# Two-layer decoder trunk on one core: the low halves of the query weights and of two up-weight chunks move from VectorE to GpSimd

## Chip, cores and metric

One core of one Trainium2 chip runs the whole kernel. The metric is device time in microseconds for one launch. The unchanged kernel was measured three times: median 3047.41 us (3045.8 to 3048.99).

## The reference, cut to what matters

512 tokens of width 1024 go through two layers. Each layer is a mixer (three parallel head groups, then an output projection added to x) and then a PEER block: 16384 one-neuron experts, of which each token uses 128, chosen by eight product-key heads.

```
x = x + mixed @ w_out[i]
xn = rmsnorm(x, norm_ffn[i])
q = (xn @ w_q)                      # 1024 x 2048: 16 blocks of 128 columns
s1, s2 = q halves against keys1, keys2      # 128 keys each
v1, i1 = top_k(s1, 16); v2, i2 = top_k(s2, 16)
... 16 best sums per head -> experts, gates = softmax
h = gelu(u[experts] . xn)           # u: 128 chunks of 128 experts
x = x + sum(gates * h * v[experts])
```

## The kernel before, in words

Products that must be exact to float32 are made of three passes on TensorE (`mm3`, L75 to L77): high times high (L75), high times low (L76), low times high (L77). So each weight block of 128x1024 is split in two: ScalarE rounds it to the high half (`uh`, L650), VectorE subtracts that from the block for the low half (`ul`, L651). Only L77 reads `ul`.

At the end of a layer's mixer, TensorE makes the output projection (`pso`) block of 128 tokens by block. For each block VectorE adds the result to x (L369), ScalarE takes the sum of squares (`sq`, L173), VectorE works out the reciprocal root in a chain of twelve 128x1 instructions (L161 to L168) and scales the block (`xn`, L185), TensorE transposes it (`psn`, L189), and ScalarE and VectorE split it again (`ahi`, L191; `alo`, L192). The last add and norm, those of tokens 384 to 511, are the generator `rest`, which the PEER part starts.

The PEER part loads three of the sixteen query blocks (numbered c = -16 to -14), splits them, and runs them at once against the first 256 tokens (`qmm`, `psq` of 128x256), while the norm of the last tokens is still under way. Then it goes through the sixteen query blocks: half or all of the product, scores against the keys (`pss`, L677), and on VectorE `best` (L892 to L896: the 16 best of 128 for each token, four blocks of tokens, some 80 instructions for each query block). The same stream of blocks then goes on with c = 0, 1, ... 127, the chunks of u (`hidden`, `psh` of 128x384); `uraw`, `uh` and `ul` have three buffers each. From there VectorE also does the routing (`route`), the gate matrices, and the rows of the last token block, which GpSimd gathers (L735).

The order on each engine is set by a scheduler, which orders by readiness and priority. What is wrapped in `pin` (`keep_in_program_order`) keeps the order of the program among the pinned instructions of its own engine. The `uh` and `ul` of the first three query blocks are pinned, and so is the last add of x:

```python
            split_u(-NQ)
            split_u(1 - NQ)
            split_u(2 - NQ)
            next(rest)          # tc.keep_in_program_order(add(*late))
            first = [self.psA.tile([P, T], F32, tag="a", name="psq") for _ in range(3)]
            for j in range(3):
                qmm(j, first[j], slice(0, T // 2))
            next(rest, None)    # norm of the last 128 tokens
```

So on VectorE that add (L369) stands behind three `ul`. An engine takes its instructions strictly in its own order.

Of the kernel before, what the change touches and what calls it, by code (L numbers as in the profile page):

```python
# [7 lines left out]
F32 = mybir.dt.float32  # L8
F32R = mybir.dt.float32r
# [5 lines left out]
OP = mybir.AluOpType  # L15
# [4 lines left out]
P = 128  # L20
# [3 lines left out]
KD = D // P  # L24
# [14 lines left out]
NUW = 3  # L39
# [24 lines left out]
class K:  # L64
# [562 lines left out]
    def peer(self, L, xh, xl, rest):  # L627
        nc, tc, ins = self.nc, self.tc, self.ins
        G = self.dr.tile([NCH // GE, P, TD // TBAT, GE * TBAT], F32, tag="G", name="G")
        H = self.dr.tile([NPRE, P, TD], F32, tag="H", name="H")  # L630
        with ExitStack() as pc:
# [6 lines left out]
            pin = tc.keep_in_program_order  # L638
            gt, us, uw, vs, hs = {}, {}, {}, {}, {}
# [6 lines left out]
                    us[c] = self.up.tile([P, KD, P], F32, tag="uraw", name="uraw", bufs=NUR)  # L646
                    pin(nc.sync.dma_start(us[c], ins["peer_u"][L, c] if c >= 0 else ins["peer_w_q"][L, c + NQ]))

            def split(hi, lo, src, pin=pin):
                pin(nc.scalar.copy(hi, src))  # L650
                self.last = pin(nc.vector.tensor_tensor(lo, src, hi.bitcast(F32), op=OP.subtract))  # L651
                return hi, lo

            def split_u(c, pin=pin):
                if c < NCH:
                    uw[c] = split(self.up.tile([P, KD, P], F32R, tag="uh", name="uh", bufs=NUW),
                                  self.up.tile([P, KD, P], F32R, tag="ul", name="ul", bufs=NUW), us.pop(c), pin)

            def hidden(c, pin=pin):
                uh, ul = uw.pop(c)  # L660
# [30 lines left out]
            for j in range(3):  # L691
                load_u(j - NQ)
# [3 lines that stand above are left out]
            next(rest)  # L696
            first = [self.psA.tile([P, T], F32, tag="a", name="psq") for _ in range(3)]
# [371 lines left out]
```

## Time and profile before

| what | value |
|---|---|
| median of 3 runs | 3047.41 us |
| profiled execution, its own time | 3044.03 us |
| its span | 3042.3 us |
| TensorE busy | 2971.3 us, 98% |
| VectorE busy | 2443.7 us, 80% |
| ScalarE busy | 1268.9 us, 42% |
| GpSimd busy | 736.2 us, 24% |
| mean granted TensorE clock | 0.993 |

All times within the program are microseconds from the start of the span. The PEER part of layer 0 begins at about 286, that of layer 1 at about 1796. A granted clock of 1.00 stands for 2.4 GHz and 0.50 for 1.2 GHz; a value between them is a window that holds some of both.

### The profile page before, as it was taken

Reading aid. Unit: us, or ns where it says so; the run is one execution under the profiler, and the core shown is the slowest. Engines: PE = TensorE matmul, PEld = TensorE weight load, DVE = VectorE, ACT = ScalarE, POOL = GpSimd, SP = SyncE. Lnnn points to the kernel's source line nnn. Section 1 sums busy time; section 2 is a strip of 40 time slices with the busy share of each in tenths; the row PEclk is TensorE's granted clock in tenths of the full one; section 3 lists DMA queues with packets and bytes.
Section 4 is the critical chain, followed back from the end, with each engine's and each line's share of the span. In section 5 each row is a group of like instructions: output and inputs, shape, how many; then the busy total and the mean of one; then the engine's idle time right before and its main releaser. Section 6 shows DMA issues by size and latency. Waiting matters only on the chain.

```text
span 3042.3 us, 45583 instructions
## 1 busy us (share of the span) xinstructions
PE 2971.3 (98%) x16742; PEld 2659.7 (87%) x16742; DVE 2443.7 (80%) x5057; ACT 1268.9 (42%) x1874; POOL 736.2 (24%) x553
## 2 busy tenths in 40 slices
PE   7999999999999999999999999999999999999998
PEld 7977889999999998788889788999999999988886
DVE  5766999987788787877766769999868788878777
ACT  5343346556333333333353533555553333323333
POOL 0000000222455544322100000002225555542221
PEclk9999999999999999999999999999999999999999
DMA  4212247799989888999722212578999899889996
GB/s 122 67 58 70 98 143 255 271 307 335 348 321 333 322 324 309 362 335 330 282 78 67 73 65 96 169 242 295 314 351 335 323 321 338 330 295 353 333 348 232
DMA packets 335696, 756.64 MB, mean 249 GB/s; under 512 B 31568, under 2 KB 192240, under 8 KB 331376
## 3 DMA queue, kind: packets, MB, share of 16 engines
q1 hardware_dynamic: 141936, 406.60, 37.2%
q0 software_dynamic: 73728, 268.47, 24.7%
q10 hardware_dynamic: 119808, 78.66, 8.2%
q8 instruction: 131, 2.15, 0.3%
q14 instruction: 93, 0.76, 0.1%
HBM read 672.89 MB, written 80.74 MB: 248 GB/s over the span
## 4 chain that ended last, share of the span: by engine, by line
PE 79%; DVE 6%; issue 4%; ACT 4%; DMA 3%; POOL 2%; ACTq 1%; SPq 0%; POOLq 0%; DVEq 0%
PE pv L77 10%; PE pv L76 10%; PE pv L75 10%; PE psh L75 9%; PE psh L77 9%; PE psh L76 9%; PE psp L77 2%; PE psp L76 2%; PE psp L75 2%; PE psq L76 2%; PE psq L77 2%; PE psq L75 2%; POOL row L735 2%; DMA row<-in_v_rows,idx 1%; ACTq L789 1%
## 5 line engine op out<-in xcount | busy, mean ns | idle before, releaser
L735 POOL DMA_INDIRECT row<-in_u_rows,idx x256 | 389.1, 1520 | 1326.3 <-DVE si L893 679.3
L75 PE MATMUL psh<-ahi,uh 128*128 128x384 f32 x2048 | 694.5, 339 | 10.1 <-ACT ht L665 10.1
L77 PE MATMUL psh<-ahi,ul 128*128 128x384 f32 x2048 | 689.2, 337 | 6.6 <-DVE ul L651 6.6
L76 PE MATMUL psh<-alo,uh 128*128 128x384 f32 x2048 | 688.4, 336 | 0.0
L75 PE MATMUL pv<-vh,wh 128*128 128x512 f32 x1536 | 597.7, 390 | 10.4 <-ACT wh L835 10.4
L77 PE MATMUL pv<-vh,wl 128*128 128x512 f32 x1536 | 600.4, 391 | 0.0
L76 PE MATMUL pv<-vl,wh 128*128 128x512 f32 x1536 | 599.9, 391 | 0.0
L735 POOL DMA_INDIRECT row<-in_v_rows,idx x256 | 329.1, 1286 | 604.1 <-DVE yacc L752 568.3
L650 ACT CAST uh<-uraw 128x1024 fp32r<-128x1024 f32 x288 | 302.7, 1053 | 319.8 <-PE psh L76 154.4
L651 DVE TENSOR_TENSOR ul<-uraw,uh 128x1024 fp32r<-128x1024 f32 x288 | 350.4, 1220 | 98.9 <-ACT uh L650 85.5
L75 PEld LDWEIGHTS psh<-ahi,uh 128*128 128x128 f32 x2048 | 387.1, 189 | 16.2 <-ACT ht L665 11.9
L77 PEld LDWEIGHTS psh<-ahi,ul 128*128 128x128 f32 x2048 | 386.6, 189 | 7.2 <-DVE ul L651 7.2
L76 PEld LDWEIGHTS psh<-alo,uh 128*128 128x128 f32 x2048 | 387.0, 189 | 4.1
L821 DVE TENSOR_TENSOR vl<-vraw,vh 128x1024 fp32r<-128x1024 f32 x256 | 312.5, 1221 | 86.5 <-issue 66.5
L665 ACT ACTIVATE ht<-psh 128x384 f32<-128x384 f32 x256 | 125.3, 489 | 613.6 <-PE psh L77 601.1
L75 PEld LDWEIGHTS pv<-vh,wh 128*128 128x128 f32 x1536 | 288.9, 188 | 69.3 <-ACT wh L835 12.0
L77 PEld LDWEIGHTS pv<-vh,wl 128*128 128x128 f32 x1536 | 288.9, 188 | 61.6 <-DVE wl L821 1.1
L76 PEld LDWEIGHTS pv<-vl,wh 128*128 128x128 f32 x1536 | 289.0, 188 | 58.6 <-DVE vl L821 0.5
L752 DVE SCALAR_TENSOR_TENSOR yacc<-row,wk,yacc 128x1024 f32<-128x1024 f32 x254 | 325.7, 1282 | 11.0 <-DMA row<-in_v_rows,idx 9.5
L743 DVE SCALAR_TENSOR_TENSOR gscr<-row,xg 128x1024 f32<-128x1024 f32 x256 | 312.5, 1221 | 13.0 <-DMA row<-in_u_rows,idx 11.3
L835 ACT CAST wh<-ht 128x384 fp32r<-128x384 f32 x256 | 130.7, 510 | 383.2 <-PE pv L76 236.3
L826 ACT CAST vh<-vraw 128x1024 fp32r<-128x1024 f32 x256 | 268.7, 1050 | 26.6 <-DMA vraw<-in_v_rows 24.5
(289 smaller groups left out, 4406.8 us busy)
## 6 DMA issues: line engine op xcount, KB each, us to landing
uraw<-in_peer_u SPq DMA_DIRECT2D x256, 512.0 KB
vraw<-in_v_rows SPq DMA_DIRECT2D x256, 512.0 KB
G<-stg ACTq DMA_DIRECT2D x48, 1024.0 KB
g<-G SPq DMA_DIRECT2D x32, 1536.0 KB
H<-ht ACTq DMA_DIRECT2D x144, 192.0 KB
ht<-H SPq DMA_DIRECT2D x144, 192.0 KB
wraw<-in_w_in SPq DMA_DIRECT2D x96, 256.0 KB
uraw<-in_peer_w_q SPq DMA_DIRECT2D x32, 512.0 KB
```

Of the source, the lines that this page charges most:

```text
L75: mm(ps, ah, bh, start=first, stop=False)
L76: mm(ps, ah, bl, start=False, stop=False)
L77: mm(ps, al, bh, start=False, stop=last)
L650: pin(nc.scalar.copy(hi, src))
L651: self.last = pin(nc.vector.tensor_tensor(lo, src, hi.bitcast(F32), op=OP.subtract))
L665: pin(nc.scalar.activation(hs[c], ps, AF.Gelu))
L735: nc.gpsimd.indirect_dma_start(out=r, out_offset=None, in_=ins[name], in_offset=bass.IndirectOffsetOnAxis(ap=idx[:, k:k + 1], axis=0))
L743: nc.vector.scalar_tensor_tensor(sc, r, 1.0, xg, op0=OP.mult, op1=OP.mult, accum_out=hd[:, k:k + 1])
L752: nc.vector.scalar_tensor_tensor(yacc, r, wk[:, k:k + 1], yacc, op0=OP.mult, op1=OP.add)
L821: self.last = pin(nc.vector.tensor_tensor(lo, src, hi.bitcast(F32), op=OP.subtract))
L826: pin(nc.scalar.copy(vh[c], vs[c]))
L835: pin(nc.scalar.copy(wh[c], hs[c]))
```

## The change

`split` takes the engine of the subtraction as an argument, and `split_u` gives GpSimd for c below 2: the sixteen query blocks and the u chunks 0 and 1. That is 18 subtractions in each layer, 36 in all. ScalarE still makes the high halves.

```diff
-            def split(hi, lo, src, pin=pin):
+            def split(hi, lo, src, pin=pin, eng=nc.vector):
                 pin(nc.scalar.copy(hi, src))
-                self.last = pin(nc.vector.tensor_tensor(lo, src, hi.bitcast(F32), op=OP.subtract))
+                self.last = pin(eng.tensor_tensor(lo, src, hi.bitcast(F32), op=OP.subtract))
                 return hi, lo
...
-                                  self.up.tile([P, KD, P], F32R, tag="ul", name="ul", bufs=NUW), us.pop(c), pin)
+                                  self.up.tile([P, KD, P], F32R, tag="ul", name="ul", bufs=NUW), us.pop(c), pin,
+                                  nc.gpsimd if c < 2 else nc.vector)
```

On GpSimd the 18 instructions of a layer stand in one row between the last memset of the mixer and the first gather. SyncE's order doesn't change. On VectorE the 18 are gone, and all others stand in the order they had. On VectorE at the start of the PEER part (layer 0; layer 1 alike), where `x<-x,pso` is the add of the last 512 columns of the last tokens:

```order
 L369 TENSOR_TENSOR x<-x,pso 128x512
 L192 TENSOR_TENSOR alo<-psn,ahi 128x4x128 x2
-L651 TENSOR_TENSOR ul<-uraw,uh 128x1024 x3
 L369 TENSOR_TENSOR x<-x,pso 128x512
 L161 TENSOR_SCALAR rv<-ss 128x1
```

The last add no longer stands behind three subtractions. On ScalarE at the same place, where `sq` is the sum of squares of the last tokens and the three `uh` are the first query blocks:

```order
 L173 ACTIVATE sq,ss<-x 128x1024
 L191 CAST ahi<-psn 128x4x128 x2
+L173 ACTIVATE sq,ss<-x 128x1024
 L650 CAST uh<-uraw 128x1024 x3
-L173 ACTIVATE sq,ss<-x 128x1024
 L191 CAST ahi<-psn 128x4x128 x2
 L650 CAST uh<-uraw 128x1024
```

The scheduler now puts the sum of squares ahead of the three high halves instead of behind them. On TensorE, at the first query block, where `psn` is a transpose of the last tokens' `xn`:

```order
 L75 MATMUL psq<-ahi,uh 128x256
 L76 MATMUL psq<-alo,uh 128x256
+L189 MATMUL psn<-ident,xn_2670 128x128
 L77 MATMUL psq<-ahi,ul 128x256
 L75 MATMUL psq<-ahi,uh 128x256
```

One of the eight transposes of the last tokens now stands between the second and the third matmul of the first query block; the other seven stay where they were, behind the first pass over the three blocks. These are all the differences on TensorE and ScalarE, and they are the same in both layers.

## Rows read from the trace of the kernel before

**Rows 1.** The page's part 1: busy time of an engine, its share of the span, instructions.
```profile
PE 2971.3 (98%) x16742; PEld 2659.7 (87%) x16742; DVE 2443.7 (80%) x5057; ACT 1268.9 (42%) x1874; POOL 736.2 (24%) x553
```

**Rows 2.** The table of waits of TensorE, whole span: who waited for whom, us in total, times, the longest.
```profile
PE pv L75 <- ACT wh L835: 10.4, 4, 4.6
PE psh L75 <- ACT ht L665: 10.1, 5, 3.3
PE psh L77 <- DVE ul L651: 6.6, 2, 3.3
...
PE psq L77 <- DVE ul L651: 1.8, 2, 0.9
```

**Rows 3.** Busy time in two stretches of the query stage of layer 0: PE, PEld, DVE, ACT, POOL (with instructions), granted clock, DMA share, GB/s.
```profile
310.00:330.00 20.00, 20.00 (x101) 16.29 (x100) 20.00 (x111) 6.73 (x10) 0.00 (x0) 1.00 0.19 72
...
350.00:370.00 20.00, 20.00 (x102) 16.53 (x101) 19.75 (x107) 6.69 (x10) 0.00 (x0) 1.00 0.24 79
```

**Rows 4.** Timeline of VectorE through the end of the query stage: start, duration, operation, in brackets the idle time before it and who ended it. The last row is layer 1.
```profile
370.30 0.49 DVE L892 MAX8 V<-sc 128x8 f32<-128x128 f32 x2 [0.55 <-ACT sc L679]
...
394.32 1.21 DVE L651 TENSOR_TENSOR ul<-uraw,uh 128x1024 fp32r<-128x1024 f32 x1
396.08 0.49 DVE L892 MAX8 V<-sc 128x8 f32<-128x128 f32 x2 [0.56 <-ACT sc L679]
...
408.71 1.22 DVE L651 TENSOR_TENSOR ul<-uraw,uh 128x1024 fp32r<-128x1024 f32 x1
...
1905.84 0.49 DVE L892 MAX8 V<-sc 128x8 f32<-128x128 f32 x2 [0.56 <-ACT sc L679]
```

**Rows 5.** Timeline of TensorE just behind the query stage of layer 0: the two waits there.
```profile
409.98 0.44 PE L77 MATMUL psh<-ahi,ul 128*128 128x384 f32 x1 [3.28 <-DVE ul L651]
...
416.98 0.45 PE L75 MATMUL psh<-ahi,uh 128*128 128x384 f32 x1 [1.00 <-ACT ht L665]
```

**Rows 6.** Timeline of ScalarE at the start of the PEER part of layer 0: the sum of squares of tokens 256 to 383, then the three high halves.
```profile
274.95 1.06 ACT L173 ACTIVATE sq<-x 128x1024 f32<-128x1024 f32 x1 [4.31 <-DVE x L369]
275.92 0.18 ACT L173 ACTIVATION_READ_ACCUMULATOR sq<-x 128x1 f32 x1
...
281.51 2.96 ACT L650 CAST uh<-uraw 128x1024 fp32r<-128x1024 f32 x3
```

**Rows 7.** Timeline of VectorE at the same place: add, start of the root's chain and scaling for tokens 256 to 383, the three low halves, then the same for tokens 384 to 511.
```profile
274.17 0.69 DVE L369 TENSOR_TENSOR x<-x,pso 128x512 f32<-128x512 f32 x1 [2.80 <-PE pso L77]
276.13 0.15 DVE L161 TENSOR_SCALAR rv<-ss 128x1 f32<-128x1 f32 x1 [1.28 <-ACT sq L173]
...
278.45 1.28 DVE L185 SCALAR_TENSOR_TENSOR xn<-x,ry,grow 128x1024 f32<-128x1024 f32 x1
...
286.33 3.50 DVE L651 TENSOR_TENSOR ul<-uraw,uh 128x1024 fp32r<-128x1024 f32 x3 [3.87 <-issue]
289.74 0.68 DVE L369 TENSOR_TENSOR x<-x,pso 128x512 f32<-128x512 f32 x1
...
293.63 0.16 DVE L167 SCALAR_TENSOR_TENSOR rt<-rt,rv 128x1 f32<-128x1 f32 x1
293.82 0.16 DVE L168 SCALAR_TENSOR_TENSOR ry<-rt,ry 128x1 f32<-128x1 f32 x1
...
294.09 1.28 DVE L185 SCALAR_TENSOR_TENSOR xn<-x,ry,grow 128x1024 f32<-128x1024 f32 x1
```

**Rows 8.** Timeline of TensorE at the same place: the last matmul of the projection of tokens 256 to 383 and their first transposes; the last matmul of the projection; the first query block; the end of the first pass over three blocks.
```profile
273.73 0.40 PE L77 MATMUL pso<-woh,ml 128*128 128x512 f32 x1
...
279.88 1.07 PE L189 MATMUL psn<-ident,xn 128*128 128x128 f32 x8 [0.23 <-DVE xn L185]
...
286.07 0.39 PE L77 MATMUL pso<-woh,ml 128*128 128x512 f32 x1
286.30 0.28 PE L75 MATMUL psq<-ahi,uh 128*128 128x256 f32 x1
286.42 0.28 PE L76 MATMUL psq<-alo,uh 128*128 128x256 f32 x1
287.61 0.39 PE L77 MATMUL psq<-ahi,ul 128*128 128x256 f32 x1 [0.91 <-DVE ul L651]
...
295.99 0.28 PE L77 MATMUL psq<-ahi,ul 128*128 128x256 f32 x1
```

**Rows 9.** The same place in layer 1: VectorE and TensorE.
```profile
1796.08 3.50 DVE L651 TENSOR_TENSOR ul<-uraw,uh 128x1024 fp32r<-128x1024 f32 x3 [3.88 <-issue]
1797.35 0.39 PE L77 MATMUL psq<-ahi,ul 128*128 128x256 f32 x1 [0.91 <-DVE ul L651]
```

**Rows 10.** Busy time in windows of 2 us, columns as in Rows 3, behind two waits of TensorE: that of 3.28 us that ended at 409.98, and the longest of Rows 2, 4.6 us, that ended at about 2729.
```profile
410.00:412.00 2.00, 2.00 (x7) 2.00 (x8) 2.00 (x1) 1.51 (x3) 0.00 (x0) 0.61 0.28 90
412.00:414.00 2.00, 2.00 (x8) 2.00 (x8) 2.00 (x5) 0.00 (x0) 0.00 (x0) 0.53 0.71 270
...
2728.00:2730.00 2.00, 0.68 (x2) 0.59 (x3) 2.00 (x4) 1.24 (x2) 1.01 (x1) 0.53 0.73 261
2730.00:2732.00 2.00, 2.00 (x6) 1.59 (x5) 1.96 (x3) 0.22 (x1) 0.28 (x1) 0.50 0.86 244
2732.00:2734.00 2.00, 2.00 (x6) 1.58 (x5) 1.97 (x2) 0.00 (x0) 1.70 (x2) 0.50 0.89 335
2734.00:2736.00 2.00, 2.00 (x8) 1.59 (x8) 2.00 (x4) 1.27 (x2) 1.70 (x2) 0.77 0.81 281
```

**Rows 11.** Groups of instructions by line and shape: GpSimd's memset of a tile of 128x1024, and VectorE's low halves: count, busy us, mean ns of one, idle before.
```profile
L325 POOL MEMSET qz<- 128x1024 f32 x4 | 3.7, 954 | 88.8 <-PE pg L619 88.8
```
```profile
L651 DVE TENSOR_TENSOR ul<-uraw,uh 128x1024 fp32r<-128x1024 f32 x288 | 350.4, 1220 | 98.9 <-ACT uh L650 85.5
```

## Prediction

> **What bounds the kernel now.** I read the page's busy times first: TensorE is busy 98% of the span, VectorE 80% [rows 1]. So an edit off TensorE is worth only what it does to TensorE's waits, and the next view is the table of those waits [rows 2]: low halves are waited for twice 3.3 us at `psh` and twice 0.9 us at `psq`. The third view is the stage that loses work from VectorE. In the query stage VectorE is as good as full (20.00 of 20 us), and so is TensorE (20.00 of 20) [rows 3]. A full VectorE invites the thought that the stage waits for it. The timeline says otherwise: from 370 on, each search for the best 16 starts only after VectorE has stood idle 0.55 us for ScalarE's `sc` [rows 4], and `sc` comes from TensorE. VectorE keeps up, with about half a microsecond to spare for each block, and TensorE never stops in the stage.
>
> **What the change gives.** Per layer it takes 18 x 1.22 = 22 us from VectorE [rows 11]. In the query stage this only makes that idle time longer. Just behind it stand two waits of TensorE, 3.28 and 1.00 us [rows 5]. The first ends with the `ul` at 408.71 [rows 4]. Which chunk is that? Counting the low halves of the layer on VectorE, it is the twentieth, so c = 3, and that one stays on VectorE: the change takes c up to 1. It comes at the end of an unbroken row of VectorE work that begins at 396.08, when `sc` of the last query block arrives [rows 4], so its distance from TensorE's own end of the query stage stays 12.6 us. The subtraction that ends at 395.53 (c = 2, likewise unmoved) was done before `sc` came. I take the gain there as 0. In layer 1 the last search waits 0.56 us for `sc` too [rows 4]. The moved low halves of this stage have cover: a block takes 6.4 us (four searches from 370.30 to 396.08 [rows 4]), the three buffers let a block be split one block ahead of its matmuls, and GpSimd has nothing else to do until the gathers.
>
> **What it costs: the start of the PEER part.** Here all edits meet, and the orders decide. Before: ScalarE makes three high halves from 281.51, while TensorE is still in the projection [rows 6]; TensorE goes on to the query blocks at 286.30 without a break, stops 0.91 us for the first low half, and restarts at 287.61 [rows 8]. After: ScalarE's order has the last tokens' `sq` ahead of the high halves, and `sq` waits for the last add of x, which waits for the last matmul of the projection. What was ready 2 us early now begins behind it. Step by step, with the distances of the preceding token block:
> - The last projection matmul starts at 286.07 [rows 8]. An add starts 0.44 us behind such a matmul (273.73 to 274.17) [rows 7, 8]: add at 286.51.
> - `sq` starts 0.78 behind the add, its accumulator read ends 1.93 behind it [rows 6, 7]: 288.44. The first high half, about 1 us (2.96 for three) [rows 6]: 289.4. TensorE's first query matmul starts there, not at 286.30: a wait of 3.1 us, then 0.25 us of work.
> - Next in TensorE's order is the moved transpose. It needs `xn`. The root's chain starts 1.96 behind the add, `xn` 4.35 (289.74 to 294.09), and the transpose 1.43 behind that (278.45 to 279.88) [rows 7, 8]: 286.51 + 4.35 + 1.43 = 292.3. A second wait, 2.6 us.
> - The third matmul also needs the first low half from GpSimd. No row shows that operation there. From below: what VectorE takes, 1.22 us; from above: a memset of that shape on GpSimd is 0.95 us, and three passes (two reads, one write) at that pace are 2.86 [rows 11]. I take 2.86, worked out from GpSimd's own row, the nearest: 289.5 + 2.86 = 292.4. Within both ends the transpose is as late, so the sum doesn't move. The second and third low halves come at 295.3 and 298.2, ahead of their blocks (a block's pass is 2.9 us, 8.38 for the three from 287.61 to 295.99 [rows 8]).
> - TensorE so restarts at 292.4 instead of 287.61: 4.8 us later.
>
> The Trainium skill (GPSIMD Engine Reference, Performance versus the Vector engine) gives 4.5 us for a GpSimd add of 2048 float32, so an estimate of 2.25 us for 1024; no row here shows one, and by it the sum would be the same.
>
> The clock adds to this. Behind a wait of 3.28 us TensorE was granted 0.61 and 0.53 for two windows of 2 us, that is, most of them at 1.2 GHz: 0.78 + 0.94 = 1.7 us of work lost. Behind a wait of 4.6 us the loss is 2.8 (0.34 for the 0.68 us at work in the first window, then 1.0, 1.0 and 0.46) [rows 10]. Two waits of 3.1 and 2.6 us with two matmuls between lie near these; the bounds are 0 and 2.8, I take 1.7, as the single wait is nearer in length. Nothing else changes there: the seven other transposes and the second pass follow in the old order, and 0.1 us is saved since one transpose has been made.
>
> Sum: 4.8 + 1.7 - 0.1 = 6.4 us in layer 0, and the same in layer 1, where order and rows are alike [rows 9]. TensorE is busy without slack behind both places, and VectorE, the loads and the gathers start from what TensorE and ScalarE deliver, so nothing takes up the delay: 12.8 us. On the profiled execution's 3044.03 us that is 3056.8; the median of the runs lies 3.4 us above that execution, so the forecast is **3060 us**. With no drop of the clock it is 3047.4 + 9.4 = 3056.8.
>
> **Rivals.**
> 1. *VectorE and GpSimd get in each other's way at the same place: slower still.* No row shows a GpSimd operation that reads two tiles, so the trace speaks neither for nor against. From 289.5 on, GpSimd would run three subtractions in a row, until 289.5 + 3 x 2.86 = 298.1. In just that time VectorE goes through the second half of the root's chain, small two-input instructions 0.19 us apart (293.63, 293.82), and `xn`, also of two tiles [rows 7]. If an instruction of VectorE with two inputs has to wait until a running GpSimd one ends, at most one or two slip in between two of them, and after 298.1 about four small ones, a copy and `xn` remain: 2.1 us. TensorE then restarts at 300.3, 12.7 us late, with 2.8 for the clock: 15.5 in a layer, 31 in all, **3078 us**. At 1.22 us for one subtraction it would be 295.3, 7.7 + 1.7 in a layer, 3066. The Trainium skill (SBUF — State Buffer, Who interferes with whom) states just this: a VectorE instruction with two SBUF inputs and a GpSimd one that reads SBUF exclude each other for a whole instruction. Chance 0.35.
> 2. *The relief of VectorE counts: faster.* If the row of VectorE work behind the query stage began earlier, the waits of 3.28 and 1.00 us and the clock's 1.7 behind them would go: 6.0 us in a layer, 12 in all, and were there no new wait at the start, 3047.4 - 12 = **3035 us**. The point from which it decides: VectorE must reach the last search later than its `sc`. It is 0.56 us early in both layers [rows 4], so I give this 0.04. Together with the new wait at the start it comes to 3047.4 + 12.8 - 12 = 3048, no change.
> 3. *It doesn't cost what the order says: no change, about 3049.* That could be if a later wait took up the delay: the transfers behind some of `psh`'s waits for `ht` [rows 2] could run on while TensorE stands. But buffers bound how far ahead the loads run, and they come free through TensorE. With rival 2's second case: 0.09.
>
> **How the numbers follow.** Forecast 0.52 (3055 to 3064, its ends being the clock's two bounds), rival 1 0.35 (3066 to 3078), rival 2 0.04, rival 3 and the mixed case 0.09. The range reaches from just below the forecast without a clock drop, 3054, to rival 1 at its dear end with 2 us for the spread of the runs, 3080; what is left out is the 0.13 below and some 0.05 above (a subtraction on GpSimd of over 3 us). A measurement of this kernel can tell about 0.2%, 6 us, from no change. Slower by more than that: 0.52 + 0.35 = 0.87; faster 0.04; within 0.09.
>
> **What would show it.** In the changed profile: in both layers ScalarE's first `uh` some 7 us later than before, near 288.4 instead of 281.5; TensorE's first query matmul near 289.4 behind a wait of about 3 us, then a second wait named for `xn` or `ul`, and a restart at 292 to 293 (forecast) or near 300 (rival 1, with gaps of a GpSimd instruction's length inside the chain of 128x1 instructions); a granted clock near 0.5 for some 3 us behind it; the query stage's VectorE share down from 20.00 to about 16 of 20 with TensorE unchanged; the wait of 3.3 us behind the query stage still there for `ul`, with the same 12.6 us from the last `sc`. What would make the prediction wrong: `uh` made before `sq` after all; that 3.3 us wait gone; or GpSimd so slow that low halves are waited for in the query stage, from about 6.4 us each.

## The result, and the profile after

The changed kernel takes 3072.69 us in the median of six runs (3068.33 to 3076.62), the kernel before beside it 3047.38 (3045.8 to 3049.76): ratio 1.0082, 95% interval 1.0069 to 1.0095, 25 us slower. The profiled execution took 3073.22 us, with a span of 3071.4 and a mean granted clock of 0.988.

The page's part 1, as in [rows 1]:

```profile
PE 2978.7 (97%) x16742; PEld 2662.0 (87%) x16742; DVE 2416.4 (79%) x5021; ACT 1268.4 (41%) x1874; POOL 824.5 (27%) x589
```

VectorE ran 36 instructions fewer, 36 x 1.22 = 44 us of work, and yet its busy time fell by only 2443.7 - 2416.4 = 27 us. Some of its instructions became longer. The table of TensorE's waits, as in [rows 2], says who is waited for now:

```profile
PE psn L189 <- DVE xn L185: 17.1, 4, 8.3
...
PE psh L77 <- DVE ul L651: 8.8, 6, 3.3
...
PE psq L75 <- ACT uh L650: 5.9, 2, 3.0
```

Two waits of 3.0 us for the high halves are new, and so are two of 8.3 us for `xn`; the two of 3.3 us for `ul` at `psh` are still there. The next views show layer 0's start of the PEER part, where the new waits are. First the timeline of VectorE (compare [rows 7]):

```profile
285.73 0.69 DVE L369 TENSOR_TENSOR x<-x,pso 128x512 f32<-128x512 f32 x1 [4.04 <-PE pso L77]
...
288.84 2.21 DVE L166 TENSOR_TENSOR rt<-ry 128x1 f32<-128x1 f32 x1
291.08 2.26 DVE L167 SCALAR_TENSOR_TENSOR rt<-rt,rv 128x1 f32<-128x1 f32 x1
293.38 2.26 DVE L168 SCALAR_TENSOR_TENSOR ry<-rt,ry 128x1 f32<-128x1 f32 x1
295.67 0.16 DVE L166 TENSOR_TENSOR rt<-ry 128x1 f32<-128x1 f32 x1
...
296.33 1.28 DVE L185 SCALAR_TENSOR_TENSOR xn<-x,ry,grow 128x1024 f32<-128x1024 f32 x1
```

Timeline of GpSimd at the same place, and one subtraction by itself in the query stage:

```profile
288.68 6.95 POOL L651 TENSOR_TENSOR ul<-uraw,uh 128x1024 fp32r<-128x1024 f32 x3 [124.60 <-DVE rt L167]
...
341.85 2.38 POOL L651 TENSOR_TENSOR ul<-uraw,uh 128x1024 fp32r<-128x1024 f32 x1 [4.13 <-ACT uh L650]
```

Instructions on 128 x 1 numbers, which take 0.16 us by themselves, take 2.2: three of them, exactly while GpSimd makes its three low halves (288.68 to 295.63). One instruction of VectorE gets in each time a subtraction ends. `xn` so begins 296.33 - 285.73 = 10.60 us behind the add instead of 4.35.

Timeline of ScalarE (compare [rows 6]):

```profile
286.51 1.06 ACT L173 ACTIVATE sq<-x 128x1024 f32<-128x1024 f32 x1 [5.66 <-DVE x L369]
...
287.57 2.92 ACT L650 CAST uh<-uraw 128x1024 fp32r<-128x1024 f32 x3
```

Timeline of TensorE (compare [rows 8]):

```profile
285.30 0.39 PE L77 MATMUL pso<-woh,ml 128*128 128x512 f32 x1
288.65 0.56 PE L75 MATMUL psq<-ahi,uh 128*128 128x256 f32 x1 [2.95 <-ACT uh L650]
...
297.75 0.45 PE L189 MATMUL psn<-ident,xn 128*128 128x128 f32 x1 [8.33 <-DVE xn L185]
...
308.30 0.93 PE L189 MATMUL psn<-ident,xn 128*128 128x128 f32 x7
```

The high halves come behind `sq`, TensorE waits 2.95 us for the first, does two matmuls, and stands 8.33 us at the moved transpose. In the kernel before, the transposes behind the first pass were in this row:

```profile
296.11 1.03 PE L189 MATMUL psn<-ident,xn 128*128 128x128 f32 x8
```

From the last projection matmul to these transposes it was 296.11 - 286.07 = 10.04 us; it is 308.30 - 285.30 = 23.00. The clock adds its part, in windows of 2 us (columns as in [rows 3]):

```profile
298.00:300.00 2.00, 2.00 (x11) 2.00 (x11) 0.00 (x0) 0.00 (x0) 0.00 (x0) 0.50 0.21 80
...
302.00:304.00 2.00, 2.00 (x18) 2.00 (x17) 0.00 (x0) 0.00 (x0) 0.00 (x0) 0.91 0.00 0
```

TensorE restarts at 1.2 GHz and is back at 2.4 GHz after some 4.5 us. The pass from restart to transposes takes 10.55 us instead of 8.50: 2.05 more, nearly all of it the clock's (the moved transpose takes up 0.1 of it). Layer 1 is alike: 22.75 instead of 10.03. So the two places cost 12.96 + 12.72 = 25.7 us, as much as the 25.3 by which the medians differ. (The two profiled executions, from which these rows are, lie 29.1 us apart in span; where the other 3.4 are isn't shown.)

The end of the query stage on VectorE (compare [rows 4]):

```profile
402.51 0.49 DVE L893 MAX8 V<-sc 128x8 f32<-128x128 f32 x2 [1.71 <-ACT sc L680]
...
408.99 0.49 DVE L893 MAX8 V<-sc 128x8 f32<-128x128 f32 x2 [0.58 <-ACT sc L680]
...
421.60 1.22 DVE L651 TENSOR_TENSOR ul<-uraw,uh 128x1024 fp32r<-128x1024 f32 x1
```

The wait of TensorE just behind it (compare [rows 5]):

```profile
422.87 0.69 PE L77 MATMUL psh<-ahi,ul 128*128 128x384 f32 x1 [3.26 <-DVE ul L651]
```

What VectorE was spared became idle time: once the stage is under way it stands idle 1.7 us ahead of a search, where it stood 0.55. Only ahead of the last search it is 0.58, since the low half of c = 2, which VectorE still makes, comes just before. From the last `sc` to the low half of c = 3 it is 421.60 - 408.99 = 12.6 us, as before, and the wait behind it is the same 3.3 us.

### The profile page after: what moved, and what is told of

It reads as the page before. It is cut to its first block, busy times and chain, and to the rows that moved or that the text cites. A ratio compares the mean times of both kernels' runs of the same rounds, so it can differ in the third digit from the quotient of the medians.

```text
span 3071.4 us, 45581 instructions
## 1 busy us (share of the span) xinstructions
PE 2978.7 (97%) x16742; PEld 2662.0 (87%) x16742; DVE 2416.4 (79%) x5021; ACT 1268.4 (41%) x1874; POOL 824.5 (27%) x589
## 4 chain that ended last, share of the span: by engine, by line
PE 69%; DVE 14%; issue 7%; DMA 3%; POOL 3%; ACT 3%; ACTq 1%; SPq 0%; POOLq 0%; DVEq 0%
PE pv L77 9%; PE pv L75 9%; PE pv L76 9%; PE psh L75 7%; PE psh L77 7%; PE psh L76 7%; POOL row L736 3%; PE psp L77 2%; PE psp L76 2%; PE psp L75 2%; PE psq L76 2%; PE psq L77 2%; PE psq L75 2%; DVE ul L651 2%; DMA row<-in_v_rows,idx 2%
## 5 line engine op out<-in xcount | busy, mean ns | idle before, releaser
L77 PEld LDWEIGHTS psh<-ahi,ul 128*128 128x128 f32 x2048 | 386.6, 189 | 10.9 <-DVE ul L651 10.9
L651 DVE TENSOR_TENSOR ul<-uraw,uh 128x1024 fp32r<-128x1024 f32 x252 | 307.4, 1221 | 88.1 <-ACT uh L650 84.5
```

Of the source, the lines that this page charges most:

```text
L77: mm(ps, al, bh, start=False, stop=last)
L651: self.last = pin(eng.tensor_tensor(lo, src, hi.bitcast(F32), op=OP.subtract))
```

## Experiments

The theory after the result: the loss is all at the start of the PEER part and has two causes that act together. ScalarE makes the first high halves late, behind `sq`; and the three subtractions on GpSimd, one behind the other, hold up the two-input instructions of the root's chain on VectorE, for which TensorE now waits in the middle of the first query block. The rivals: the loss comes from the other 15 subtractions of a layer; or the instructions of 2.2 us are not held up by GpSimd; or the late high halves alone are enough. "Head" below is the time from TensorE's last projection matmul to the transposes of the last tokens behind the first pass; it is 10.04 us in the kernel before.

**1. The other fifteen.** The first three stay on VectorE.

```diff
-nc.gpsimd if c < 2 else nc.vector)
+nc.gpsimd if 3 - NQ <= c < 2 else nc.vector)
```


> GpSimd makes 15 of the 18 low halves of a layer; those of the first three query blocks are back on VectorE, and with them the orders of ScalarE and TensorE are those of before. Theory A (the whole loss arises at the start of the PEER part; in the query stage neither engine gains or costs anything): the start as before, TensorE waits 0.9 us there, and 3047 us, within 3 us of the kernel before. Rival (VectorE's relief counts): the waits of 3.3 and 1.0 us behind the query stage shrink, 3035 to 3041. Rival (GpSimd's 2.4 us for a subtraction is too slow somewhere in the query stage): waits for ul at psq, 3053 or more.

Measured: 3045.24 us against 3044.68, ratio 1.0001 (0.9992 to 1.0010). Head 10.03 us. The thirty subtractions of the query stage cost nothing and bring nothing. TensorE's timeline has both waits for `ul` as the kernel before has them:

```profile
286.95 0.39 PE L77 MATMUL psq<-ahi,ul 128*128 128x256 f32 x1 [0.91 <-DVE ul L651]
...
410.08 0.69 PE L77 MATMUL psh<-ahi,ul 128*128 128x384 f32 x1 [3.25 <-DVE ul L651]
```

**2. The first three alone.**

```diff
-nc.gpsimd if c < 2 else nc.vector)
+nc.gpsimd if c < 3 - NQ else nc.vector)
```


> GpSimd makes only the low halves of the first three query blocks (6 of the 36 in both layers); the other 30 are back on VectorE. All orders as in the changed kernel. Theory A (the loss sits at the start of the PEER part alone): the whole loss of the changed kernel, 23 to 28 us over the kernel before. Rival (the loss is spread over all GpSimd subtractions): a sixth of it, 4 to 5 us.

Measured: 3071.10 us against 3045.11, ratio 1.0088 (1.0073 to 1.0104). Head 22.87 us in layer 0, 23.37 in layer 1. Six of the 36 subtractions make the whole loss.

**3. The high halves early again.** All 18 on GpSimd, and the last sum of squares pinned, so that it stays behind the three `uh` on ScalarE; the transpose goes back behind the pass by itself.

```diff
+        sqi = self.nc.scalar.activation(sq, self.x[:, tb], AF.Square, accum_out=ss)
+        if pinned:
+            self.tc.keep_in_program_order(sqi)
```


> All 18 low halves on GpSimd as in the changed kernel, but the last sum of squares is pinned behind the three high halves; ScalarE's and TensorE's orders are those of before again. Theory A (GpSimd's subtractions hold up VectorE's two-input instructions, and TensorE pays because the high halves come late and a transpose of the last tokens stands in the middle of its first block): the chain of the root is still stretched, by one or two instructions of some 2.3 us, but hidden under the first pass; TensorE waits about 2.2 us for the first low half instead of 0.9, 3050 us (3053 if the clock drops behind it). Rival (GpSimd's use alone is what costs, whatever the order): 3070 or more.

Measured: 3052.71 us against 3044.68, ratio 1.0022 (1.0011 to 1.0032). Timeline of VectorE:

```profile
287.65 2.05 DVE L166 TENSOR_TENSOR rt<-ry 128x1 f32<-128x1 f32 x1
289.74 2.30 DVE L167 SCALAR_TENSOR_TENSOR rt<-rt,rv 128x1 f32<-128x1 f32 x1
```

Timeline of GpSimd:

```profile
285.00 7.02 POOL L653 TENSOR_TENSOR ul<-uraw,uh 128x1024 fp32r<-128x1024 f32 x3 [121.70 <-PE pso L76]
```

Timeline of TensorE, the wait for the first low half and the transposes:

```profile
287.41 0.39 PE L77 MATMUL psq<-ahi,ul 128*128 128x256 f32 x1 [2.09 <-POOL ul L653]
...
297.40 1.03 PE L191 MATMUL psn<-ident,xn 128*128 128x128 f32 x8
```

GpSimd's three start at 285.00, and the two chain instructions that fall beside the last two are held up; but nobody waits for the chain now, since the transposes come 10 us later. What is left is the slower low half: a wait of 2.09 us instead of 0.91, and the clock behind it (0.50 granted from 288 to 290 and 0.70 from 290 to 292, where the kernel before has 1.00). Head 12.7 us, 2 x 2.7 = 5.3 of the 8 measured; the other 2.7 are open.

**4. High halves late, transposes back.** Orders as in the changed kernel, but the transposes of the last tokens are pinned behind the last matmul of the first pass.

```diff
+                    tp = nc.tensor.transpose(ps[:, i], xn[:, (kk + i) * P:(kk + i + 1) * P], self.ident)
+                    if keep is not None and tb == TB - 1:
+                        self.tc.keep_in_program_order(tp)
...
+                if n.stop == T // 2:
+                    pin(e)
```


> As the changed kernel, but the one moved transpose stands behind the first pass again, with the other seven. Theory A: VectorE's chain is stretched as before (three instructions of 2.2 us), but TensorE no longer waits for it in the first block; it waits for the first high half (about 3 us) and then for the first low half (about 2.3), and the first pass ends 4 to 7 us later than in the kernel before, in each layer: 3056 to 3061. Rival (the stretched chain costs wherever the transpose stands): 3070 or more. Rival (late high halves are nothing, the transpose is all): 3048 to 3050.

Measured: 3060.93 us against 3044.68, ratio 1.0052 (1.0037 to 1.0068). Timeline of TensorE:

```profile
289.16 0.56 PE L75 MATMUL psq<-ahi,uh 128*128 128x256 f32 x1 [2.96 <-ACT uh L652]
...
291.60 0.58 PE L77 MATMUL psq<-ahi,ul 128*128 128x256 f32 x1 [1.67 <-POOL ul L653]
...
302.02 1.04 PE L189 MATMUL psn<-ident,xn 128*128 128x128 f32 x8
```

The chain is held up as in the changed kernel (three instructions of 2.2 to 2.3 us), `xn` begins at 296.92, and that is early enough. Head 16.21 and 16.25 us: the late high halves and the slower low half cost 6.2 us in a layer. The moved transpose, which makes TensorE wait for the held-up chain, costs the other 23.0 - 16.2 = 6.8. Of the 16.2 us measured, 12.4 lie in the two heads; the other 3.9 are open.

**5. Shorter instructions on GpSimd.** This kernel leaves out the first three subtractions: in their place GpSimd copies the high half into the low half, one operand in the place of two. Orders as in the changed kernel.

```diff
-self.last = pin(eng.tensor_tensor(lo, src, hi.bitcast(F32), op=OP.subtract))
+self.last = pin(nc.gpsimd.tensor_copy(lo, hi.bitcast(F32)) if c < 3 - NQ else eng.tensor_tensor(lo, src, hi.bitcast(F32), op=OP.subtract))
```


> As the changed kernel, with the same orders on all engines, but for the first three query blocks GpSimd makes a cast of the high half in place of the subtraction (one input instead of two; the low halves of these three blocks are left wrong). Theory A1 (any GpSimd instruction that reads a tile shuts out VectorE's two-input instructions): some instructions of the chain are stretched to the length of the cast, about three if it takes 1 to 1.5 us, TensorE restarts 3 to 4 us earlier than in the changed kernel, 3062 to 3067. Theory A2 (only GpSimd's second input is in the way): the chain is not stretched, TensorE restarts about 6 us behind the last projection matmul instead of 12.4, 3058 to 3060. Rival (the engines don't hinder each other, the chain is long for another reason): 3072.

Measured: 3063.91 us against 3044.68, ratio 1.0060 (1.0045 to 1.0076). Timeline of GpSimd:

```profile
288.69 3.02 POOL L651 CAST ul<-uh 128x1024 fp32r<-128x1024 f32 x3 [124.64 <-DVE rt L167]
```

Timeline of VectorE:

```profile
288.87 0.88 DVE L166 TENSOR_TENSOR rt<-ry 128x1 f32<-128x1 f32 x1
289.78 0.95 DVE L167 SCALAR_TENSOR_TENSOR rt<-rt,rv 128x1 f32<-128x1 f32 x1
290.77 0.95 DVE L168 SCALAR_TENSOR_TENSOR ry<-rt,ry 128x1 f32<-128x1 f32 x1
```

TensorE at the moved transpose:

```profile
293.82 0.45 PE L189 MATMUL psn<-ident,xn 128*128 128x128 f32 x1 [4.64 <-DVE xn L185]
```

Again three instructions are held up, now for 0.9 us each, the length of a copy. So it isn't the second operand on GpSimd that matters, it is the length of its instruction; a copy that reads one tile does the same. The wait at the transpose falls from 8.33 to 4.64, and the heads, 18.36 and 19.37 us, have 17.7 of the 19.2 measured.

**6. The chain with one tile as input.** The nine instructions of L166 to L168 for the last tokens become `tensor_scalar`, with the other operand as a number for each partition. Here the transposes go back behind the pass as well.

```diff
+                nc.vector.tensor_scalar(t, y, y, None, op0=OP.mult)
+                nc.vector.tensor_scalar(t, t, -0.5, v, op0=OP.mult, op1=OP.mult)
+                nc.vector.tensor_scalar(y, t, 1.5, y, op0=OP.add, op1=OP.mult)
```


> All 18 low halves on GpSimd; in the root's chain of the last tokens the nine two-input instructions take their second operand as a per-partition scalar, so each has one tensor input. The scheduler puts the moved transpose back behind the first pass. Theory A (only VectorE instructions with two tensor inputs are shut out): all nine take about 0.16 us while GpSimd subtracts, none 2.2; xn, which has two tensor inputs, is stretched by up to 2.3 us instead; the time is that of the kernel with the transpose back, 13 to 17 us over the kernel before, as there TensorE doesn't wait for the chain. Rival (GpSimd's subtraction slows any VectorE instruction): the same stretched rows of 2.2 us.

Measured in a single execution: 3063.65 us, against a median of 3045.11. Timeline of VectorE:

```profile
289.62 0.21 DVE L169 TENSOR_SCALAR ry<-rt,ry 128x1 f32<-128x1 f32 x1
...
291.11 0.21 DVE L169 TENSOR_SCALAR ry<-rt,ry 128x1 f32<-128x1 f32 x1
...
291.43 1.55 DVE L190 SCALAR_TENSOR_TENSOR xn<-x,ry,grow 128x1024 f32<-128x1024 f32 x1
```

Timeline of GpSimd:

```profile
289.54 8.01 POOL L656 TENSOR_TENSOR ul<-uraw,uh 128x1024 fp32r<-128x1024 f32 x3 [124.58 <-ACT uh L655]
```

While GpSimd subtracts, seven of these instructions pass in 0.21 us each. The hold-up is one of instructions with two tiles as input, and it goes both ways: beside the two-input `xn`, GpSimd's three took 8.01 us instead of 6.95. As in experiment 4 nobody waits for the chain here, so the head is about the same, 16.51 and 16.45 us, and the time is no better than that kernel's; (6.47 + 6.42) = 12.9 of the 18.5 us lie in the heads, and where the other 5.6 are, in this one execution, is open.

**7. Further up-weight chunks.** The first three stay on VectorE. If the wait of 3.3 us behind the query stage hangs on the low half of c = 3, moving that one must remove it.

```diff
-nc.gpsimd if c < 2 else nc.vector)
+nc.gpsimd if 3 - NQ <= c < 8 else nc.vector)      # from_four_to_eight
+nc.gpsimd if 3 - NQ <= c < 16 else nc.vector)     # from_four_to_sixteen
```


> GpSimd makes the low halves of the later 13 query blocks and of u chunks 0 to 7; the first three query blocks stay on VectorE. Theory A: the wait of 3.3 us for the low half of chunk 3 behind the query stage goes in both layers, and with it the clock's drop; but VectorE's routing instructions there have two tensor inputs and are held up by GpSimd's subtractions, so a later wait takes part of it: 3 to 8 us faster than the kernel before. Rival (nothing else waits behind that): 10 to 12 us faster. Rival (the held-up routing costs more than the wait): no change or slower.

> As the former, with u chunks 0 to 15 on GpSimd. Theory A: the same first wait goes, but twice as many subtractions run against the two-input routing instructions, which decide when the gate matrices and the gathers begin: between 8 us faster and 3 us slower than the kernel before, and not better than with 8 chunks. Rival (VectorE's relief counts there): better than with 8 chunks by 3 us or more.

Measured against 3045.11: 3058.84 us, ratio 1.0049 (1.0035 to 1.0063), and 3099.41 us, ratio 1.0185 (1.0172 to 1.0199). Both slower, where the theory had a gain of some us from c = 3, with the heads as before (10.03 us). Of the kernel with c below 8, three rows of VectorE in the routing, and the routing's result `ex` for which TensorE waits below:

```profile
412.24 3.30 DVE L947 TENSOR_TENSOR pr<-ge,dstart 128x2048 f16<-128x2048 f16 x1
415.46 2.48 DVE L923 TENSOR_TENSOR gt<-gt,zs 128x128 f32<-128x128 f32 x1
417.87 3.43 DVE L941 TENSOR_TENSOR pr<-pr 128x2048 f16<-128x2048 f16 x1
...
429.35 0.38 DVE L942 TENSOR_TENSOR ex<-pr 128x128 f32<-128x128 f16 x1
```

The same rows in the kernel before:

```profile
413.49 1.17 DVE L946 TENSOR_TENSOR pr<-ge,dstart 128x2048 f16<-128x2048 f16 x1
414.58 0.28 DVE L922 TENSOR_TENSOR gt<-gt,zs 128x128 f32<-128x128 f32 x1
...
417.05 1.22 DVE L940 TENSOR_TENSOR pr<-pr 128x2048 f16<-128x2048 f16 x1
...
430.44 0.38 DVE L941 TENSOR_TENSOR ex<-pr 128x128 f32<-128x128 f16 x1
```

GpSimd beside them:

```profile
411.50 8.72 POOL L651 TENSOR_TENSOR ul<-uraw,uh 128x1024 fp32r<-128x1024 f32 x3 [6.56 <-ACT uh L650]
```

TensorE behind the query stage, its waits of over 0.6 us for these:

```profile
410.54 0.44 PE L75 MATMUL psh<-ahi,uh 128*128 128x384 f32 x1 [0.70 <-ACT ht L666]
...
429.79 0.48 PE L965 MATMUL rtr<-ident,ex 128*128 128x128 f32 x1 [5.74 <-DVE ex L942]
...
488.55 0.45 PE L77 MATMUL psh<-ahi,ul 128*128 128x384 f32 x1 [3.02 <-DVE ul L651]
```

The wait of 3.3 us is gone: c = 3 was indeed the chunk. After the first seven chunks (168 matmuls) TensorE is 4.6 us ahead of the kernel before, counted from the last projection matmul (284.55 here, 286.07 there). Beside the subtractions from c = 4 on, the routing's instructions are held up, each of the three rows by some 2.2 us. But VectorE is also spared low halves there, and the `ex` of the rows comes no later in the end: 145.2 us behind the last projection matmul instead of 144.8. TensorE waits 5.74 us for it because it is ahead, and because the scheduler changed TensorE's order: the transpose of this `ex` stands behind 168 matmuls of the chunks, where it stood behind 174. The gain from c = 3 so runs into the routing. The order of VectorE behind the query stage changed too, and the 3.02 us at 488.55 are a wait for a low half that VectorE made in the midst of its other work, when GpSimd had made its last one long before (at 420.2). The time from the last projection matmul of layer 0 to that of layer 1 grows by 9.0 us with c below 8 and by 29.9 with c below 16, where the same `ex` comes 4.6 us later than in the kernel before. How much of this the held-up instructions cost and how much the new orders, these two runs can't tell.

**8. Only the chunk that is waited for.** c = 2 and 3 alone, and those from the fourth query block to c = 3.

```diff
-nc.gpsimd if c < 2 else nc.vector)
+nc.gpsimd if 2 <= c < 4 else nc.vector)           # chunks_two_and_three
+nc.gpsimd if 3 - NQ <= c < 4 else nc.vector)      # from_four_to_three
```


> Only the low halves of the u chunks c = 2 and 3 go to GpSimd (two in each layer); all others, the query blocks among them, stay on VectorE. Theory A (a subtraction on GpSimd is worth something where TensorE waits for that very low half and where no two-input instruction of VectorE that is soon waited for runs beside it): the low half of c = 3 is then made near 402.5 to 405, as in the run with c up to 7 on GpSimd, instead of at 408.71 to 409.9; the wait of 3.28 us behind the query stage and the 1.7 us of lost clock behind it go in both layers, a wait of 0.7 us for ht takes the first one's place: 2 x (3.28 + 1.7 - 0.7) = 8.6 us faster, 3036 to 3038 against 3045. Rival B (that wait only hides a later one, of the routing or of ht, which then grows by as much): within 3 us of the kernel before.

> The low halves of the query blocks from the fourth on and of the u chunks 0 to 3 go to GpSimd (17 in each layer); the first three and all from c = 4 on stay on VectorE. Theory A (the loss in the run with c up to 7 came from the subtractions of c = 4 to 7, beside which the routing's two-input instructions had to wait, and its gain from c = 3): as with c = 2 and 3 alone, 3036 to 3038. Rival B (the held-up instructions in the query stage, the gate's scaling and the sums of the candidates, cost as much as is won): 3042 to 3048. Rival C (the routing is late for other reasons): near 3058, as with c up to 7.

Measured against 3045.77: 3043.74 us, ratio 0.9994 (0.9985 to 1.0003), and 3045.49 us, ratio 0.9997 (0.9988 to 1.0006). No gain that can be told from none. Here TensorE's order behind the query stage of layer 0 is that of the kernel before, in both runs. Timeline of TensorE with c = 2 and 3 alone:

```profile
410.17 0.45 PE L75 MATMUL psh<-ahi,uh 128*128 128x384 f32 x1 [0.64 <-ACT ht L666]
411.50 0.44 PE L75 MATMUL psh<-ahi,uh 128*128 128x384 f32 x1 [0.70 <-ACT ht L666]
414.44 0.69 PE L77 MATMUL psh<-ahi,ul 128*128 128x384 f32 x1 [2.34 <-DVE ul L651]
```

Instead of 3.28 and 1.00 us [rows 5] TensorE waits 0.64, 0.70 and 2.34: 3.68 instead of 4.28. The next chunk that VectorE makes, c = 4, stands behind the same search and the routing's first instructions, and is now the one waited for, again with the clock at 1.2 GHz behind it (0.50 granted from 414 to 418). Theory A falls in both runs. In the second the three waits are 0.69, 0.72 and 2.33, so it is c = 4 again, and not the query stage, that takes the gain.

## Why the prediction was right, and which term was mis-sized

The direction and the place held, and 3072.7 lies in the stated range of 3054 to 3080. The forecast's own number did not hold: 3060 has half of the loss, 12.6 us of 25.3, and its band of 3055 to 3064 was missed. (The clock's two bounds alone give 3056.8 and 3062.4, so the band was already some 1.7 us wider on either side than its working.) The range held because it reached over rival 1, and it is rival 1's mechanism that the runs show. Point by point:

- *Relief of VectorE worth 0:* held. 1.71 us of idle time ahead of a search, the same 12.6 us to c = 3, the same wait of 3.3 us, and experiment 1 measures the thirty later subtractions by themselves at nothing. VectorE's share of a window, said to fall to about 16 of 20 us, fell to 14.32 from 350 to 370: in the kernel before, VectorE was still working off a backlog there, and stood idle ahead of a search only from 370 on [rows 4]. (From 310 to 330 it is 14.17, but there VectorE first stands idle until 316.56, because the whole stage starts later.) The mechanism held, the size was off, with no effect on the time.
- *High halves behind `sq`:* held step by step. Add 0.43 us behind the last projection matmul (0.44 said), first query matmul behind a wait of 2.95 (3.1). Experiment 4 measures the late start with the clock, without the moved transpose, at 6.2 us in a layer's head, where the forecast had 6.4 (16 us in all instead of 12.8, of which 3.9 lie outside the heads); TensorE's restart there, 291.60 - 285.81 = 5.79 us behind the last projection matmul, is 4.25 late (4.8 said).
- *The subtraction on GpSimd:* 2.38 us, between the bounds of 1.22 and 2.86, and nearer to the latter, which was taken. The page GPSIMD Engine Reference of the Trainium skill (Performance versus the Vector engine), by which an estimate of 2.25 stood in the prediction, was near.
- *Clock, 1.7 in a layer:* 2.05 measured, between the bounds; the wait it follows was longer.
- *The step that failed:* "It needs `xn`. ... 286.51 + 4.35 + 1.43 = 292.3: a second wait, 2.6 us." The 4.35 us from the add to `xn` were 10.60. The difference, 6.25, is that of three rows: 2.21 + 2.26 + 2.26 against 3 x 0.16. The other two terms of that step held (`xn` to transpose 1.42). So the second wait was 8.33 us, and TensorE restarted 12.45 us behind the last projection matmul instead of 1.54, 10.9 us later where the forecast had 4.8.
- *Rival 1, given 0.35, is what happened.* With the measured 2.38 us its own working gives 289.5 + 3 x 2.38 + 2.1 = 298.7, 11.1 us late (10.9 measured); with 2.05 for the clock 13.2 in a layer, 26.3 in all, 3047.4 + 26.3 = 3073.7; measured 3072.7. It said that at most one or two small instructions slip in between two subtractions: it was one each time. The Trainium skill's rule (SBUF — State Buffer, Who interferes with whom), cited there, agrees with the trace: 0.16 us became 2.2 beside a subtraction of 2.38 us, 0.9 beside a copy of 1.0; and the same section's exception for instructions with at most one SBUF input, outside the modes that use both ports, agrees with the 0.21 us of experiment 6. The forecast left the rule a chance below that of the case in which nothing is shared, on the ground that no row showed a GpSimd instruction that reads two tiles. No row spoke against it either.
- *Rival 2 (relief counts):* its point of decision was that VectorE must be behind its `sc`; it isn't. Experiment 8 shows more: even with the low half of c = 3 made in time, a wait for c = 4 takes the place of most of it; and in experiment 7, where c = 4 too is made in time, TensorE waits for the routing.
- *Rival 3 (a later wait takes up the delay):* fell. The heads' 25.7 us and the measured 25.3 are the same.

## What to carry to other kernels

Before work with two tiles, or a copy, goes to GpSimd, look at what two-input instructions VectorE has to do in just that time, small ones above all: each instruction of a dependent chain that meets a running GpSimd one can cost that one's whole length, whatever its own size; if nobody waits for that chain, it costs nothing. A wait that is removed can come back at the next thing in the row (the low half of c = 4 in experiment 8, the routing in experiment 7): follow the row of work behind it, not the one instruction that the table of waits names. And an edit on one engine can change the scheduler's order on two others: here pinning ScalarE's alone took the loss from 25 to 8 us, and pinning TensorE's alone to 16.

## What the runs showed that was not expected

- GpSimd's copy of 128x1024, with one tile read, held up VectorE's small two-input instructions just as the subtraction did: 0.88 to 0.95 us for a copy of 1.0 us. Exactly one instruction of VectorE passed between two of GpSimd's that followed each other, in all five kernels whose chain ran beside GpSimd's subtractions or copies (the changed one and experiments 2 to 5).
- The hold-up is mutual: beside one two-input instruction of VectorE of 128x1024, three subtractions of GpSimd took 8.01 us instead of 6.95.
- An operand given as a number for each partition isn't held up, and costs 0.05 us more for 128 x 1: 0.21 us instead of 0.16.
